# Sparse attention: TensorE's instructions of the heads held in the order of the program

## The chip, the cores and the metric

The kernel runs on one core of a Trainium2 chip. The metric is the device time of one execution in microseconds (us). The engines are TensorE (PE; its weight loads are listed apart as PEld), VectorE (DVE), ScalarE (ACT), GpSimd (POOL) and SyncE (SP), which here issues the DMAs.

## What is computed

A decoder trunk of two layers, for 256 tokens of 1024 features in float32. Layer 0 is half a SwiGLU step, stick-breaking attention, and half a SwiGLU step. Then one set of keys and values for sparse attention is derived. Layer 1 is half a SwiGLU step, native sparse attention with 16 query heads over 4 groups of keys and values, and half a SwiGLU step. The part that matters here is the sparse attention:

```python
proj = hn @ w_in
q = _apply_rope(_rmsnorm(proj[..., :H * Dh], q_norm), cos, sin)
gates = jax.nn.sigmoid(proj[..., H * Dh:])
p_c = softmax(where(valid_c, q @ k_c, NEG))       # 15 compressed keys
o_s = _nsa_selected(q, sel_idx, k_s, v_s)         # selected blocks
o_w = _nsa_window(q, k_w, v_w)                    # window of 512 keys
o = gates[0] * (p_c @ v_c) + gates[1] * o_s + gates[2] * o_w
h = h + o @ w_out
```

With 256 tokens there are four blocks of 64 keys and up to eight may be selected, and the window is longer than the sequence, so the selected and the window branch both attend causally to all keys, each with keys and values of its own.

## The kernel before

**Number format.** Products of float32 are made of three matmuls of the type fp32r (`mm3`, lines 159 to 162): each operand is split into a high part, the rounded copy made by ACT, and a low part, the remainder made by DVE. Weights arrive by DMA in units of 128 x 1024, and `pump` (L114, L116) splits a unit ahead of its use.

**What sets the order.** The program is written with a tile framework. Each instruction is traced with the tiles that it reads and writes; a scheduler then puts the instructions of each engine into one fixed order, by its own model of when each is ready and by a priority that follows the order of tracing. Semaphores are added behind that. On the chip every engine works through its fixed list; an instruction that has to wait holds what stands behind it. A tile taken from a pool with a tag and a number of buffers waits until an earlier occupant of the buffer has been read for the last time. PSUM has eight banks: the tag `acc` has four, `z` two and `aux` two.

**The sparse attention, `nsa`.** The queries and gates are projected in three blocks (`proj_block`, tile `qp`). The 16 heads, in groups `sc` of four, then pass through these steps:

- `q_trans` (L950 on): for a pair of heads, four transposes into one `aux` bank (tile `qTp`, L958), which ACT copies to `qs` (L960).
- `scores(n)`: eight matmuls (L973) into two banks. They hold a mask, the scores of 16 compressed keys, of the selected branch and of the window branch. DVE takes maxima and scales them (L990 to L993); ACT makes the exponentials of the four parts with their sums (L996, L1001) and copies the compressed scores to `cs` (L998); DVE inverts the sums (L1005); POOL multiplies by gates (L1006) and scales the probabilities P in two multiplications (L1009). Heads 0 and 2 take banks of the tag `z`, all others two of `acc`.
- `cmp_soft(sc)`: the softmax of the compressed branch for four heads (L1015 to L1025, POOL, DVE and ACT).
- `cmp_trans(sc)`: two transposes of it into an `aux` bank (tile `ct`, L1031), evacuated by ACT and DVE (L1033, L1034).
- `ptrans(n)`: the probabilities of a head, for each of two branches (b0, b1) three transposes into an `aux` bank (tile `pt`, L1049), evacuated as a high part by ACT (L1051) and a low part by DVE (L1052) into `PT`. For every second pair of heads `PT` lies in the no longer needed tiles `hTh_m` and `hTl_m`.
- `values(k)`: six matmuls (tile `O`, lines 160 to 162 through `mm3`) for two heads and one branch; every fourth call adds six matmuls of the compressed branch and has ACT and DVE evacuate `O` to the output tile `hTh_o`, `hTl_o` (L1072, L1073).
- `chunk(k)` and `mm`: the output projection (tile `o`), eight chunks over the features, whose four accumulators `oo` take all four `acc` banks.

The order of the program behind the projection is scores(3), ptrans(1), q_trans of three pairs, scores(4), and then fifteen turns:

```python
for n in range(1, 16):
    if n == 3: q_trans(2, (5,))
    if n == 6: q_trans(2, (6, 7))
    if n % 4 == 1: cmp_soft(sc)
    if n % 4 == 3: cmp_trans(sc)
    if n + 1 < 16: ptrans(n + 1)
    if n + 4 < 16: scores(n + 4)
    if n >= 12: chunk(n - 12)
    values(n - 1)
values(15)
```

(Two lines that raise the limit of split weights and split one unit are left out here.) Before the change this order only gives the priorities: the scheduler lays single matmuls of one step between those of another. After `values(15)` come the rest of the output projection and the last SwiGLU half.

Of the kernel before, what the change touches and what calls it, by code (L numbers as in the profile page):

```python
# [16 lines left out]
P = 128  # L17
# [116 lines left out]
def build(tc, ctx, a, out):  # L134
    nc = tc.nc


    pr = ctx.enter_context(tc.tile_pool(name="pr", bufs=1, side="right"))
# [20 lines left out]
    def mm3(o, xh, xl, wh, wl, start, stop):  # L159
        nc.tensor.matmul(o, xh, wh, start=start, stop=False, skip_group_check=True)  # L160
        nc.tensor.matmul(o, xh, wl, start=False, stop=False, skip_group_check=True)  # L161
        nc.tensor.matmul(o, xl, wh, start=False, stop=stop, skip_group_check=True)  # L162
# [731 lines left out]
    def nsa(hT, rs, post, targets, st):  # L894
        kD, V, vcB = st["kD"], st["V"], st["vcB"]
        tc.keep_in_program_order(nc.scalar.preload_act_table_set("natural_log_exp_and_others"))
        with tc.tile_pool(name="ns", bufs=1) as sp:
# [6 lines left out]
            qw, Pm, PT, cs, pcT, Ox = {}, {}, {}, {}, {}, {}  # L904
            heads = [(2 * sc + i, hh) for sc in range(4) for hh in range(2) for i in range(2)]

            def q_evac(b, o):

                n = 2 * len(Q_BLOCKS[b])
                h0 = 2 * Q_BLOCKS[b][0]  # L910
                w = qw[b] = sp.tile([P, 2, 6, 2, DH], F32, tag="qw", bufs=2, name="qw")
                sq = sp.tile([P, 2, 6, DH], F32, tag="qsq", bufs=1, name="qsq")[:, :, 0:n, :]
                for t in range(2):
                    ov = o[t][:, 0:n * DH].rearrange("p (n d) -> p n d", d=DH)
                    nc.vector.scalar_tensor_tensor(w[:, t, 0:n, 1, :], ov, rs[t][:, 0:1],
                                                   st["qg"].unsqueeze(1).to_broadcast([P, n, DH]),
                                                   op0=OP.mult, op1=OP.mult)
                    nc.scalar.activation(sq[:, t], ov, AF.Square, scale=rs[t][:, 0:1])
                    if b == 0:
                        nc.scalar.activation(gt[:, t, :], o[t][:, 256:304], AF.Exp, scale=rs[t][:, 2:3])  # L920
                hi, qv = w[:, :, 0:n, 0, :], w[:, :, 0:n, 1, :]
                c, sn = [cst[:, x:x + 32].rearrange("p (t i) -> p t i", t=2).unsqueeze(2) for x in (C_COS, C_SIN)]
                t1, t2 = [sp.tile([P, 2, 6, 16], F32, tag=f"qr{i}", bufs=1, name="qr")[:, :, 0:n, :] for i in range(2)]
                nc.vector.tensor_tensor(t1, qv[:, :, :, 0:16], c.to_broadcast([P, 2, n, 16]), op=OP.mult)
                for i, j in ((0, 8), (8, 0)):
                    nc.vector.tensor_tensor(t2[:, :, :, i:i + 8], qv[:, :, :, j:j + 8],
                                            sn[:, :, :, i:i + 8].to_broadcast([P, 2, n, 8]), op=OP.mult)
                nc.vector.tensor_tensor(qv[:, :, :, 0:16], t1, t2, op=OP.add)
                nc.scalar.activation(hi.bitcast(R), qv, AF.Copy)
                nc.vector.tensor_tensor(qv, qv, hi, op=OP.subtract)  # L930
                r = rq[:, :, h0:h0 + n]

                v, y, z = [sp.tile([P, 2, 8], F32, tag=f"qn{i}", bufs=2, name="qn")[:, :, 0:n] for i in range(3)]
                nc.vector.tensor_reduce(v, sq, axis=AX.X, op=OP.add)
                nc.vector.tensor_scalar(v, v, 1.0 / DH, EPS, op0=OP.mult, op1=OP.add)
                nc.scalar.activation(y, v, AF.Ln)
                nc.scalar.activation(y, y, AF.Exp, scale=-0.5)
                nc.gpsimd.tensor_tensor(z, y, y, op=OP.mult)
                nc.gpsimd.tensor_tensor(z, z, v, op=OP.mult)
                nc.gpsimd.tensor_scalar(z, z, -0.5, 1.5, op0=OP.mult, op1=OP.add)  # L940
                nc.gpsimd.tensor_tensor(r, y, z, op=OP.mult)
                if b == 0:
                    gf = gt.rearrange("p t c -> p (t c)")
                    nc.vector.tensor_scalar(gf, gf, 1.0, None, op0=OP.add)
                    nc.vector.reciprocal(gf, gf)
                    for t in range(2):
                        gc = gt[:, t, :].rearrange("p (n r) -> p n r", r=3)[:, :, 0]
                        nc.vector.tensor_scalar(gc, gc, cst[:, C_IND + t:C_IND + t + 1], None, op0=OP.mult)

            def q_trans(b, ps_=None):  # L950
                for i, p in enumerate(Q_BLOCKS[b]):
                    if ps_ is not None and p not in ps_:
                        continue
                    a_ = aux("qTp")
                    for hh in range(2):
                        for t in range(2):
                            c = hh * 256 + t * P
                            nc.tensor.transpose(a_[:, c:c + P], qw[b][:, t, 2 * i + hh, :, :].rearrange("p x d -> p (x d)"),  # L958
                                                ident)
                    nc.scalar.activation(qs[:, 2 * p:2 * p + 2, :], a_.rearrange("p (n s) -> p n s", n=2), AF.Copy)  # L960

            def scores(n, banks=accs):
# [7 lines left out]
                sb, sa = banks("S")  # L970

                def mm(o, q, k, start=False):
                    nc.tensor.matmul(o, q, k, start=start, stop=False, skip_group_check=True)  # L973

                both = lambda k: k.rearrange("p (t c) -> p t c", t=2)[:, :, 0:256]
                sv = sb.rearrange("p (t c) -> p t c", t=2)
# [50 lines left out]
            def cmp_trans(sc):  # L1027
                a_ = aux("ct")
                e = cs[sc].rearrange("p t n i -> p t (n i)")
                for t in range(2):  # L1030
                    nc.tensor.transpose(a_[0:64, t * P:(t + 1) * P], e[:, t, :], ident)  # L1031
                x = pcT[sc] = [sp.tile([64, 256], R, tag=f"pcT{y}", bufs=1, name="pcT") for y in "hl"]
                nc.scalar.activation(x[0], a_[0:64, 0:256], AF.Copy)  # L1033
                nc.vector.tensor_tensor(x[1], a_[0:64, 0:256], x[0].bitcast(F32), op=OP.subtract)  # L1034

            def ptrans(n):
                pr = Pm.pop(n)
                m, i = divmod(n, 2)
                for b in range(2):
                    if i == 0:  # L1040
                        k = 2 * m + b
                        if k % 4 < 2:
                            PT[k] = [sp.tile([P, 768], R, tag=f"PT{y}", bufs=2, name="PT") for y in "hl"]
                        else:
                            PT[k] = [x.rearrange("p a b -> p (a b)")[:, (k % 2) * 768:(k % 2) * 768 + 768]
                                     for x in (hT[0], hT[1])]
                    a_ = aux("pt")
                    for c, s0 in ((0, b * P), (P, 256 + b * 256), (2 * P, 384 + b * 256)):
                        nc.tensor.transpose(a_[:, c:c + P], pr[:, s0:s0 + P], ident)  # L1049
                    x = [y[:, i * 384:i * 384 + 384] for y in PT[2 * m + b]]  # L1050
                    nc.scalar.activation(x[0], a_[:, 0:384], AF.Copy)  # L1051
                    nc.vector.tensor_tensor(x[1], a_[:, 0:384], x[0].bitcast(F32), op=OP.subtract)  # L1052

            def values(k):

                m, br = divmod(k, 2)
                sc, hh = divmod(m, 2)
                ag = sc // 2
                if k % 4 == 0:
                    Ox[sc] = zbank("O")  # L1060
                o = Ox[sc].rearrange("p (i s) -> p i s", i=2)
                x = [y.rearrange("p (i s) -> p i s", i=2) for y in PT.pop(k)]
                for b in range(2):
                    c = slice(0, 256) if b == 0 else slice(256, 384)
                    v = [y[:, ag, br, b, hh * 64:hh * 64 + P] for y in V]
                    mm3(o[:, :, b * P:256], v[0], v[1], x[0][:, :, c], x[1][:, :, c], k % 4 == 0 and b == 0, False)
                if k % 4 < 3:
                    return
                for i in range(2):
                    mm3(o[:, i, :], vcB[0][:, ag, i, :], vcB[1][:, ag, i, :], pcT[sc][0], pcT[sc][1], False, True)  # L1070
                hi, lo = [oT[y][:, 2 * sc:2 * sc + 2, :] for y in range(2)]
                nc.scalar.activation(hi, o, AF.Copy)  # L1072
                nc.vector.tensor_tensor(lo, o, hi.bitcast(F32), op=OP.subtract)  # L1073
# [33 lines left out]
            def chunk(k):  # L1107
# [3 lines left out]
                W.done()  # L1111
                W.pump()

            scores(3)
            ptrans(1)
            q_trans(1)
            scores(4)
            for n in range(1, 16):
# [18 lines left out]
                    chunk(n - 12)  # L1137
                values(n - 1)
            values(15)
            for k in range(4, 7):  # L1140
                for hf in range(2):
                    mm(k, 0, hf)
                W.pump()
# [171 lines left out]
```

## Time and profile before

| What | Value |
|---|---|
| median of 3 runs | 1042.96 us (1042.79 to 1043.17) |
| profiled execution, its time | 1043.2 us |
| its span, first to last instruction | 1041.1 us |
| PE busy | 1030.7 us (99%) |
| DVE, ACT, POOL busy | 659.6, 583.0, 101.5 us |
| mean granted clock of TensorE | 0.997 |
| first scores of the sparse attention | 755.3 us after the span's start |
| first pt transpose of head 1 | 772.1 us |
| last matmul of `values(15)` ends | about 838.4 us |

In the profile, a row of the timeline gives the start in us, the duration, engine, line, operation, output and inputs, shape and count; in brackets stands the idle time before it and what ended it. Matmuls overlap, and their ends are modelled, so the distance from start to start says what one costs. A row of the stretches gives, for each engine, the busy us and the number of instructions, then the granted clock of TensorE (1.00 is full), the share of time in which the DMA engines were busy, and GB/s. Line numbers are those of the kernel before.

### The profile page before, as it was taken

The page shows a single profiled execution, that of the slowest core. Times are in us where ns is not written, and L with a number is a line of the kernel's source. Part 1 is how long each engine was busy: PE and PEld are TensorE (multiplying, and loading weights), DVE is VectorE, ACT ScalarE, POOL GpSimd, SP SyncE. Part 2 cuts the span into 40 slices and gives each one's busy share as a digit, 9 for nine tenths or more (in the row PEclk, how much of TensorE's full clock was granted, in tenths as well). Part 3 has the DMA queues.
Part 4 walks back from the last instruction along what each step waited for, and adds up shares of the span by engine and source line. Part 5 has one row for each costly group of instructions (what it writes and reads, how often), then busy time and mean ns, then how long its engine had stood idle before and what let it go on. Part 6 is the DMA issues. An engine that isn't in the chain of part 4 may idle for free.

```text
span 1041.1 us, 14030 instructions
## 1 busy us (share of the span) xinstructions
PE 1030.7 (99%) x5207; PEld 866.6 (83%) x5207; DVE 659.6 (63%) x924; ACT 583.0 (56%) x939; POOL 101.5 (10%) x148
## 2 busy tenths in 40 slices
PE   9999999999999999999999999999989999999998
PEld 6888888899988888888888888888977888888887
DVE  6755554788977556544776586554888665555542
ACT  6645443687866544543665565543689745454431
POOL 0000000121100000000006310000155400000000
PEclk9999999999999999999999999999989999999999
DMA  9865666444335565565555567565440136565651
GB/s 342 270 186 181 195 188 199 161 144 142 104 119 187 179 192 184 189 192 193 165 180 181 182 209 260 176 186 158 156 141 18 42 99 221 176 191 184 187 176 41
DMA packets 51332, 178.98 MB, mean 172 GB/s; under 512 B 5824, under 2 KB 6848, under 8 KB 51264
## 3 DMA queue, kind: packets, MB, share of 16 engines
q1 hardware_dynamic: 50976, 177.93, 52.8%
q8 instruction: 41, 0.67, 0.3%
q14 instruction: 27, 0.22, 0.1%
q10 hardware_dynamic: 288, 0.16, 0.0%
HBM read 177.02 MB, written 1.05 MB: 171 GB/s over the span
## 4 chain that ended last, share of the span: by engine, by line
PE 95%; DVE 2%; ACT 1%; issue 1%; DMA 0%; SPq 0%; DVEq 0%
PE a L160 15%; PE a L162 15%; PE a L161 15%; PE o L160 9%; PE o L162 9%; PE o L161 9%; PE gTp L384 2%; PE S L973 2%; PE kv L160 1%; PE kv L162 1%; PE kv L161 1%; PE hTp L274 1%; PE a L405 1%; PE pt L1049 1%; PE b L405 1%; PE qk L515 1%
## 5 line engine op out<-in xcount | busy, mean ns | idle before, releaser
L116 DVE TENSOR_TENSOR wl<-wraw,wh 128x1024 fp32r<-128x1024 f32 (+2 forms) x330 | 402.0, 1223 | 268.0 <-ACT wh L114 259.4
L114 ACT ACTIVATE wh<-wraw 128x1024 fp32r<-128x1024 f32 (+2 forms) x332 | 346.0, 1050 | 277.2 <-PE a L162 127.7
L160 PE MATMUL a<-wh,hTh_f 128*128 128x512 f32 x528 | 209.3, 396 | 0.0
L162 PE MATMUL a<-wh,hTl_f 128*128 128x512 f32 x528 | 206.0, 390 | 0.0
L161 PE MATMUL a<-wl,hTh_f 128*128 128x512 f32 x528 | 205.8, 390 | 0.0
L162 PEld LDWEIGHTS a<-wh,hTl_f 128*128 128x128 f32 x528 | 99.1, 188 | 21.1
L161 PEld LDWEIGHTS a<-wl,hTh_f 128*128 128x128 f32 x528 | 99.3, 188 | 19.5
L160 PEld LDWEIGHTS a<-wh,hTh_f 128*128 128x128 f32 x528 | 99.2, 188 | 19.6
L376 ACT ACTIVATE sil<-a,rstd 128x256 f32<-128x256 f32 x86 | 40.9, 477 | 71.3 <-PE a L162 66.0
L160 PE MATMUL o<-wh,gTh0f 128*128 128x512 f32 x192 | 73.9, 385 | 0.0
L161 PE MATMUL o<-wl,gTh0f 128*128 128x512 f32 x192 | 73.6, 383 | 0.0
L162 PE MATMUL o<-wh,gTl0f 128*128 128x512 f32 x192 | 73.5, 383 | 0.0
L160 PE MATMUL o<-wh,gTh1f 128*128 128x512 f32 (+1 forms) x160 | 61.8, 386 | 0.0
L161 PE MATMUL o<-wl,gTh1f 128*128 128x512 f32 (+1 forms) x160 | 61.3, 383 | 0.0
L162 PE MATMUL o<-wh,gTl1f 128*128 128x512 f32 (+1 forms) x160 | 61.3, 383 | 0.0
L377 DVE SCALAR_TENSOR_TENSOR g<-a,rstd,sil 128x256 f32<-128x256 f32 x86 | 41.3, 481 | 30.9 <-ACT sil L376 30.7
L251 POOL TENSOR_TENSOR rstd<-rss,mhalf 128x1 f32<-128x1 f32 x12 | 7.7, 645 | 507.5 <-DVE rss L249 507.5
L160 PE MATMUL a<-wh,hTh 128*128 128x512 f32 x144 | 56.9, 396 | 0.0
L162 PE MATMUL a<-wh,hTl 128*128 128x512 f32 x144 | 56.0, 390 | 0.0
L161 PE MATMUL a<-wl,hTh 128*128 128x512 f32 x144 | 55.9, 390 | 0.0
L162 PEld LDWEIGHTS o<-wh,gTl0f 128*128 128x128 f32 x192 | 36.0, 188 | 7.2
L161 PEld LDWEIGHTS o<-wl,gTh0f 128*128 128x128 f32 x192 | 36.1, 188 | 7.0
(309 smaller groups left out, 1768.3 us busy)
## 6 DMA issues: line engine op xcount, KB each, us to landing
wraw<-in_f2i SPq DMA_DIRECT2D x88, 512.0 KB, 3.6
wraw<-in_f1i SPq DMA_DIRECT2D x84, 512.0 KB, 4.5
wraw<-in_f1o SPq DMA_DIRECT2D x44, 512.0 KB, 3.6
wraw<-in_f2o SPq DMA_DIRECT2D x44, 512.0 KB, 3.6
wraw<-in_sbqk SPq DMA_DIRECT2D x16, 512.0 KB, 3.5
wraw<-in_kv SPq DMA_DIRECT2D x12, 512.0 KB, 3.5
wraw<-in_sbv SPq DMA_DIRECT2D x8, 512.0 KB, 4.3
wraw<-in_sbo SPq DMA_DIRECT2D x8, 512.0 KB, 3.5
```

Of the source, the lines that this page charges most:

```text
L114: nc.scalar.activation(hi[:, 0:n], raw[:, 0:n], AF.Copy)
L116: e.tensor_tensor(lo[:, 0:n], raw[:, 0:n], hi[:, 0:n].bitcast(F32), op=OP.subtract)
L160: nc.tensor.matmul(o, xh, wh, start=start, stop=False, skip_group_check=True)
L161: nc.tensor.matmul(o, xh, wl, start=False, stop=False, skip_group_check=True)
L162: nc.tensor.matmul(o, xl, wh, start=False, stop=stop, skip_group_check=True)
L274: nc.tensor.transpose(p[:, c * P:(c + 1) * P], h[:, t, k:k + P], ident)
L376: nc.scalar.activation(sil, o[t][:, 0:256], AF.Silu, scale=rs[t][:, 0:1])
L377: nc.vector.scalar_tensor_tensor(g, o[t][:, 256:512], rs[t][:, 0:1], sil, op0=OP.mult, op1=OP.mult)
L384: nc.tensor.transpose(p[:, c * 256 + t * P:c * 256 + (t + 1) * P], gs[j, t][:, c * P:(c + 1) * P], ident)
L405: nc.tensor.matmul(o[j][t], x[:, k, t * P:(t + 1) * P], w, start=k == 0 and i == 0, stop=k == 7 and i == 2, skip_group_check=True)
L515: nc.tensor.matmul(oi, wh[:, c], xh, start=k == 0 and q == 0, stop=False, skip_group_check=True)
L973: nc.tensor.matmul(o, q, k, start=start, stop=False, skip_group_check=True)
```

## The change

A flag `order` is set while the program from `scores(3)` to `values(15)` is traced. While it is set, every matmul and transpose of these steps, and of the chunks that lie among them, passes through `tc.keep_in_program_order`. That gives the instruction an edge to the instruction traced before it on the same engine: the scheduler may not place it earlier. It is an edge for the scheduler alone; no semaphore wait comes with it. The work on other engines is traced as before and is still placed by the scheduler, and so is TensorE's work traced before and behind the flagged part. `nsa` gets an `mm3` of its own that issues the same three matmuls in the same order.

```diff
+            order = [False]
+
+            def pe(ins):
+
+                if order[0]:
+                    tc.keep_in_program_order(ins)
+                return ins
+
+            def mm3(o, xh, xl, wh, wl, start, stop):
+                for x, w, i in ((xh, wh, 0), (xh, wl, 1), (xl, wh, 2)):
+                    pe(nc.tensor.matmul(o, x, w, start=start and i == 0, stop=stop and i == 2, skip_group_check=True))
...
-                            nc.tensor.transpose(a_[:, c:c + P], qw[b][:, t, 2 * i + hh, :, :].rearrange("p x d -> p (x d)"),
-                                                ident)
+                            pe(nc.tensor.transpose(a_[:, c:c + P],
+                                                   qw[b][:, t, 2 * i + hh, :, :].rearrange("p x d -> p (x d)"), ident))
...
-                    nc.tensor.matmul(o, q, k, start=start, stop=False, skip_group_check=True)
+                    pe(nc.tensor.matmul(o, q, k, start=start, stop=False, skip_group_check=True))
...
-                    nc.tensor.transpose(a_[0:64, t * P:(t + 1) * P], e[:, t, :], ident)
+                    pe(nc.tensor.transpose(a_[0:64, t * P:(t + 1) * P], e[:, t, :], ident))
...
-                        nc.tensor.transpose(a_[:, c:c + P], pr[:, s0:s0 + P], ident)
+                        pe(nc.tensor.transpose(a_[:, c:c + P], pr[:, s0:s0 + P], ident))
...
+            order[0] = True
             scores(3)
             ptrans(1)
             q_trans(1)
...
                 values(n - 1)
             values(15)
+            order[0] = False
             for k in range(4, 7):
```

## The prediction

> **What bounds the kernel now.** I read first the page's busy times and its chain, then busy time in stretches of 6 us through the sparse attention, then TensorE's waits there, and last the timeline of single engines.
>
> ```profile
> PE 1030.7 (99%) x5207; PEld 866.6 (83%) x5207; DVE 659.6 (63%) x924; ACT 583.0 (56%) x939; POOL 101.5 (10%) x148
> ...
> PE 95%; DVE 2%; ACT 1%; issue 1%; DMA 0%; SPq 0%; DVEq 0%
> ```
>
> TensorE (PE) sets the end: time is won only where it idles or runs slowly, and lost wherever the change makes it wait. The whole kernel offers 1041.1 - 1030.7 = 10.4 us of idle time. The stretches of the heads (PE, PEld, DVE, ACT, POOL, granted clock, DMA):
>
> ```profile
> 768.00:774.00 6.00, 2.89 (x15) 1.83 (x13) 6.00 (x16) 6.00 (x20) 3.61 (x4) 0.85 0.33 109
> ...
> 786.00:792.00 6.00, 6.00 (x40) 4.64 (x39) 5.13 (x17) 5.72 (x23) 3.63 (x6) 1.00 0.00 0
> 792.00:798.00 6.00, 6.00 (x43) 5.10 (x43) 4.74 (x16) 5.80 (x23) 4.56 (x9) 1.00 0.01 1
> 798.00:804.00 6.00, 5.10 (x38) 4.09 (x37) 4.74 (x15) 5.77 (x21) 2.93 (x6) 1.00 0.00 0
> 804.00:810.00 6.00, 6.00 (x41) 4.89 (x40) 4.45 (x12) 5.70 (x23) 3.75 (x7) 1.00 0.01 3
> 810.00:816.00 6.00, 6.00 (x41) 4.95 (x39) 5.33 (x18) 4.08 (x16) 2.58 (x6) 1.00 0.00 0
> ```
>
> In the steady part PE is full in all rows but one, and ScalarE (ACT) is busy 5.7 to 5.8 of 6 us until 810. The two are almost equally loaded, so a wait of one soon reaches the other, and what keeps PE full is that the scheduler lays other ready work between the pieces of one head. The waits of PE from 750 to 850 us are few:
>
> ```profile
> PE pt L1049 <- POOL P L1009: 1.7, 1, 1.7
> PE S L973 <- ACT qsq L918: 0.8, 1, 0.8
> PE ct L1031 <- DVE hTl_m L1052: 0.6, 1, 0.6
> PE O L160 <- ACT PT L1051: 0.6, 1, 0.6
> PE O L160 <- ACT hTh_m L1051: 0.3, 1, 0.3
> ```
>
> The first two stand at the start of the pinned stretch and are followed by a slow clock:
>
> ```profile
> 771.00:772.00 1.00, 0.00 (x0) 0.00 (x0) 1.00 (x3) 1.00 (x3) 1.00 (x2) 1.00 0.52 209
> 772.00:773.00 1.00, 0.83 (x3) 0.46 (x3) 1.00 (x3) 1.00 (x6) 0.08 (x1) 0.61 0.00 0
> ...
> 778.00:779.00 1.00, 1.00 (x5) 0.82 (x5) 0.79 (x2) 0.38 (x2) 0.92 (x2) 0.50 0.67 127
> 779.00:780.00 1.00, 1.00 (x9) 0.90 (x7) 0.04 (x1) 0.60 (x1) 1.00 (x2) 0.98 0.92 377
> ```
>
> The granted clock is 0.5 until 779 and full after it. Half of about 6.3 us is 3.2 us lost.
>
> **The change part by part.** It adds no instruction and no semaphore, and moves nothing on SP, so no DMA changes place. What changes is the order on PE from scores(3) to values(15): turn n of the loop becomes [transposes of queries or of the compressed scores], the six transposes of head n+1, scores(n+4), [one chunk of the output projection], values(n-1). The first instruction that cannot go now holds back all that follows. The costs on PE, from starts to the next start:
>
> ```profile
> 795.52 0.30 PE L973 MATMUL S<-mns,identb 128*128 128x288 bf16 x1
> ...
> 796.63 0.48 PE L160 MATMUL O<-PT,Vh 128*128 128x512 f32 x1
> ...
> 797.77 0.60 PE L958 MATMUL qTp<-cst,qw 128*128 128x128 f32 x4
> 798.21 0.29 PE L973 MATMUL S<-mns,identb 128*128 128x288 bf16 x1
> ```
>
> Scores take 1.11, values 1.14, the four transposes of a query pair 0.44 us. Now one buffer of the tag aux, which has two: from its filling to its next filling.
>
> ```profile
> 802.79 0.49 PE L1049 MATMUL pt<-cst,P 128*128 128x128 f32 x3
> ...
> 804.56 0.82 PE L1049 MATMUL pt<-cst,P 128*128 128x128 f32 x6
> 805.21 0.27 PE L973 MATMUL S<-mns,identb 128*128 128x256 bf16 x1
> ```
> ```profile
> 803.38 0.49 ACT L1051 ACTIVATE PT<-pt 128x384 fp32r<-128x384 f32 x1 [0.23 <-PE pt L1049]
> ```
> ```profile
> 803.90 0.56 DVE L1052 TENSOR_TENSOR PT<-pt,PT 128x384 fp32r<-128x384 f32 x1 [0.31 <-ACT PT L1051]
> ```
>
> Six transposes take 0.65 us, so three take 0.33 and the two of ct about 0.22. The buffer turns in 804.56 - 802.79 = 1.77 us with ACT free at once. A query pair (one evacuation, no DVE step) and ct (smaller evacuations) turn in about 1.4 us, my estimate from these parts.
>
> 1. *Runs of transposes.* In the trace other work lies between them; in the new order it may not.
> - Turn 3 has qT5, ct, pt4 b0, pt4 b1 in a row. b0 needs qT5's buffer, 1.4 us after it, and PE has 0.44 + 0.22 = 0.66 of work: 0.74 wait; b1 needs ct's, at 0.44 + 1.4 = 1.84 against 1.73: 0.11.
> - Turn 6 has qT6, qT7, pt7 b0, b1: 1.4 - 0.88 = 0.52, and 0.11.
> - Turns 7 and 11 have ct, b0, b1: 1.4 - 0.22 - 0.33 = 0.85 each.
>
> Sum 0.85 + 0.63 + 1.7 = 3.2 us. (The last ct, turn 15, is followed by a chunk and costs nothing.)
>
> 2. *ACT's queue in front of the evacuations.* The 1.4 us hold for a free ACT. One head's exponentials hold it this long:
>
> ```profile
> 784.28 0.52 ACT L996 ACTIVATE P<-S,nm,rq 128x128 f32<-128x128 f32 x1
> ...
> 786.33 0.68 ACT L960 ACTIVATE qs<-qTp 128x512 fp32r<-128x512 f32 x1
> ```
>
> That is 2.05 of about 3.3 us per head (786 to 810 serves about seven heads). An evacuation meets such a block 62% of the time and waits half of it: 0.64 us, in four runs 2.5 us. Bounds: 0 (the scheduler puts the evacuation first) and 4 x 2.05 = 8.2. I take 2.5.
>
> 3. *Scores to transposes of the same head.* In the new order PE comes to pt(h) after values and two full turns from the end of scores(h): 1.14 + 2 x (0.65 + 1.11 + 1.14) = 6.9 us. In the trace of head 8:
>
> ```profile
> 788.25 0.30 PE L973 MATMUL S<-mns,identb 128*128 128x288 bf16 x1
> ...
> 789.91 0.28 PE L973 MATMUL S<-mns,identb 128*128 128x256 bf16 x1
> ```
> ```profile
> 796.19 1.61 POOL L1009 TENSOR_TENSOR P<-P,nm 128x256 f32<-128x256 f32 x2
> ```
>
> P is ready 797.80 - 790.19 = 7.6 us after its scores, while the scheduler takes its transposes at 802.79, 5 us later still. So some 0.7 us are missing in turns without extra work, about five of twelve: 3.5 us if ACT lags as now, nothing if the later scores find a shorter queue. I take a third, 1.1 us; the wait of chunk(0) for the score banks of heads 14 and 15 is the same chain without POOL and is counted in it.
>
> 4. *The start.* pt1 comes at 772.14 as before, since everything ahead of it keeps its order. So I expect the gap, and the slow clock, to stay.
>
> ```profile
> 772.14 0.83 PE L1049 MATMUL pt<-cst,P 128*128 128x128 f32 x3 [1.73 <-POOL P L1009]
> 773.55 0.79 PE L160 MATMUL O<-PT,Vh 128*128 128x512 f32 x1 [0.58 <-ACT PT L1051]
> 774.14 0.84 PE L1049 MATMUL pt<-cst,P 128*128 128x128 f32 x3
> 774.78 1.06 PE L958 MATMUL qTp<-cst,qw 128*128 128x128 f32 x4
> ...
> 779.08 0.37 PE L973 MATMUL S<-kDh,qs 128*128 128x272 f32 x1
> ```
>
> Now five fillings of aux (pt1 twice, three query pairs) stand in a row; values(0) and the first part of values(1), which lie between them today (about 1.3 us at full clock), go behind. By my estimate pt1 b1 then starts some 0.6 us sooner, the query pairs at about 774.6, 775.7 and 776.9, each a buffer's turn behind the last but one and 0.85 long at half clock, and the scores of head 4 at 778, not 779.1. That is 1.1 us sooner with 1.3 us of values owed: +0.2, and +0.5 for one evacuation behind exponentials. I take +0.7 us; bounds 0, and 1.7 if the slow stretch of 6.8 us lasts half as long again (3.4 us at half speed). [...]
>
> 5. *Waits that go.* The three later waits of the list, 0.6 + 0.6 + 0.3 = 1.5 us. Modelled ends hide more:
>
> ```profile
> 790.27 0.49 PE L1049 MATMUL pt<-cst,P 128*128 128x128 f32 x3
> 790.70 0.38 PE L160 MATMUL O<-pcT,vcBh 64*128 64x256 f32 x1
> ...
> 794.03 0.49 PE L1049 MATMUL pt<-cst,P 128*128 128x128 f32 x3
> 794.27 0.48 PE L161 MATMUL O<-PT,Vh 128*128 128x512 f32 x1
> ```
>
> The same three transposes hold PE 0.43 and 0.24 us; some six to eight such places make 1.5 us. Gain at most 3.0, taken whole.
>
> Sum: 3.2 + 2.5 + 1.1 + 0.7 - 3.0 = +4.5 us. Against the profiled execution's 1043.2 us (span 1041.1) this is 1047.7; the median of the runs, 1042.96, is 0.2 lower, so 1047.5. After the heads PE is full again and nothing gives it back.
>
> **The rivals.**
> - *Hidden anyway (no change, 1043 to 1045).* The scheduler's order already is close to the program's, and most stalls replace the 3.0 us of point 5: 3.2 + 0.7 - 3.0 = +0.9, 1043.9. For it: ACT has 2.2 us of idle in 804 to 816, so evacuations might come in time. Against: the rows before 804.
> - *Faster (1040).* With six transposes in one piece and scores always ahead of values, ACT gets its work in the order in which it is needed, evacuations never queue, and the waits of point 5 go: 1043.0 - 3.0 = 1040.0. It decides where a buffer of aux turns in less than the 0.55 to 0.88 us of transposes laid between. Against it stands the row of 1.77 us; even the shorter turns would have to be halved. A larger gain needs the gap at 769 to 772 to close, and nothing ahead of it moves.
> - *Much slower (1053).* Points 2 and 3 near their upper bounds: 3.2 + 6 + 2 + 1.7 - 3.0 = +9.9. PE and ACT then wait for each other in turn, and ACT loses in idling what it cannot make up at 95% load.
>
> **How the numbers follow.** Forecast (1045 to 1050.5) 0.47; much slower 0.15; no change 0.21; faster 0.17. About 0.2% (2.1 us) is what a measurement of this kernel can tell from none. Faster by more 0.17, within 0.21, slower 0.62. The range takes in the faster case's middle and the much slower one's: 1040.0 to 1053.5.
>
> **What would show it.** On PE: pieces in program order, no values between the transposes from 772 to 779; waits in front of the second pt of turns 7 and 11, and of pt4 and pt7, released by the DVE or ACT evacuation of ct and qT; scores(4) not before 777; clock 0.5 again from 772; the last values later by 4 to 5 us against the first pt1. I am wrong if PE's idle time in 772 to 850 does not rise by about 4 us, if the clock stays full there, or if pt waits are released by nothing but POOL.

## The result and the profile after

The changed kernel takes 1057.74 us (median of four runs, 1055.95 to 1058.57) against 1042.90 for the kernel before beside it: 14.8 us more, ratio 1.0139 [1.0123, 1.0156]. The direction was forecast, the size was not: the prediction said +4.5 and allowed for at most 1053.5.

The profiled execution took 1058.57 us, with a span of 1056.6. The page's busy times and the first line of its chain:

```profile
PE 1035.8 (98%) x5207; PEld 871.0 (82%) x5207; DVE 658.5 (62%) x924; ACT 582.6 (55%) x939; POOL 102.6 (10%) x148
...
PE 90%; DVE 3%; issue 3%; ACT 2%; POOL 1%; DMA 1%; SPq 0%; POOLq 0%; DVEq 0%; ACTq 0%
```

TensorE (PE) has the same 5207 instructions. Its idle time has grown from 10.4 to 1056.6 - 1035.8 = 20.8 us, and its busy time by 1035.8 - 1030.7 = 5.1 us. So the 15.5 us of the span are 10.4 of waiting and 5.1 of the same work done more slowly. Both stand in the stretch of the heads. The same 6 us windows as before the change (PE, PEld, DVE, ACT, POOL, granted clock, DMA):

```profile
768.00:774.00 6.00, 2.65 (x18) 1.91 (x15) 6.00 (x15) 5.95 (x22) 4.00 (x4) 0.80 0.41 135
...
786.00:792.00 6.00, 3.29 (x17) 2.60 (x14) 1.92 (x6) 3.86 (x15) 3.62 (x6) 0.73 0.02 3
792.00:798.00 6.00, 6.00 (x29) 4.99 (x28) 2.98 (x11) 2.93 (x11) 0.94 (x3) 0.71 0.00 0
798.00:804.00 6.00, 4.92 (x35) 4.12 (x34) 4.33 (x13) 3.90 (x14) 4.12 (x8) 1.00 0.01 1
804.00:810.00 6.00, 3.82 (x17) 2.94 (x16) 1.72 (x4) 3.73 (x13) 1.81 (x3) 0.65 0.00 0
810.00:816.00 6.00, 4.97 (x26) 4.06 (x25) 2.99 (x9) 3.28 (x12) 1.81 (x3) 0.78 0.01 3
...
766.00:855.00 89.00, 75.04 (x416) 61.90 (x415) 54.74 (x139) 58.95 (x191) 38.23 (x67) 0.88 0.14 43
```

The last row is the whole stretch. ScalarE (ACT), which was busy 5.7 us of each 6 until 810 before, is now busy 2.9 to 3.9 in the rows from 786 to 816, and the clock, full there before, falls to 0.65 to 0.78 in four of these five rows. In four of the five PE and ACT both idle (from 792 to 798 PE is busy throughout, but slow); the rows of turn 3 below show them waiting for each other.

PE's waits from 750 to 870 us (total, times, longest):

```profile
PE pt L1061 <- DVE pcT L1046: 4.7, 3, 2.1
PE pt L1061 <- POOL P L1021: 3.9, 2, 2.8
PE pt L1061 <- ACT qs L972: 2.7, 3, 1.9
PE qTp L970 <- DVE cm L1033: 1.1, 1, 1.1
PE pt L1061 <- DVE hTl_m L1064: 0.7, 1, 0.7
PE pt L1061 <- DVE PT L1064: 0.6, 1, 0.6
```

They sum to 13.7 us. 2.8 and 0.55 of it are at the start, where the kernel before has 0.80, 1.73 and 0.58. The other 10.3 lie in the turns, 9.3 of them in turns 3, 6, 7 and 11, the four that the prediction named. Most (4.7 + 2.7 = 7.4 us) are waits of `pt` for the copy of a buffer of `aux` that held `ct` (its low half, `pcT`) or a query pair (`qs`). Turn 3, on PE, ACT and VectorE (DVE), the columns being start, length, engine, line, operation and, in brackets, the idle time before it:

```profile
785.96 0.38 PE L1043 MATMUL ct<-cst,cs 128*64 128x128 f32 x2
786.90 0.52 PE L1061 MATMUL pt<-cst,P 128*128 128x128 f32 x3 [0.56 <-ACT qs L972]
789.57 0.90 PE L1061 MATMUL pt<-cst,P 128*128 128x128 f32 x3 [2.15 <-DVE pcT L1046]
790.26 0.45 PE L985 MATMUL S<-mns,identb 128*128 128x288 bf16 x1
```
```profile
786.16 0.60 ACT L972 ACTIVATE qs<-qTp 128x512 fp32r<-128x512 f32 x1
786.66 0.45 ACT L1008 ACTIVATE P<-S,nm,rq 128x128 f32<-128x128 f32 x1
...
788.14 0.59 ACT L1013 ACTIVATE P<-S,nm,rq 128x256 f32<-128x256 f32 x1
...
788.68 0.38 ACT L1045 ACTIVATE pcT<-ct 64x256 fp32r<-64x256 f32 x1
...
793.67 0.46 ACT L1008 ACTIVATE P<-S,nm,rq 128x128 f32<-128x128 f32 x1 [2.61 <-DVE nm L1003]
```
```profile
788.85 0.18 DVE L1017 RECIPROCAL nm<-nm 128x4 f32<-128x4 f32 x1 [2.55 <-ACT P L1013]
789.10 0.42 DVE L1046 TENSOR_TENSOR pcT<-ct,pcT 64x256 fp32r<-64x256 f32 x1
```

For comparison, the same place on PE before the change:

```profile
785.46 0.38 PE L1031 MATMUL ct<-cst,cs 128*64 128x128 f32 x2
785.68 0.29 PE L973 MATMUL S<-mns,identb 128*128 128x288 bf16 x1
...
787.33 0.49 PE L1049 MATMUL pt<-cst,P 128*128 128x128 f32 x3
```

There the scheduler lets scores follow `ct` at once, and `pt` comes 1.9 us later without a wait. The rows after the change are the whole loss in small. `ct` is done at 786.34, but its copy stands in ACT's list behind one head's exponentials, all of them, 786.66 to 788.68. On DVE the second copy stands behind a reciprocal that waits for the same exponentials. The second `pt` of turn 3 needs that buffer, and behind it, in the pinned order, stand scores that have no wait of their own when they come (790.26). PE does nothing for 2.15 us; then ACT, whose next scores come late, does nothing for 2.61.

On ACT the kernel before has the same order in this place:

```profile
786.80 0.56 ACT L996 ACTIVATE P<-S,nm,rq 128x128 f32<-128x128 f32 x1
...
788.85 0.42 ACT L1033 ACTIVATE pcT<-ct 64x256 fp32r<-64x256 f32 x1
```

There too `ct` waits for a whole head's exponentials, and its buffer is filled again only at 790.27, 4.8 us after 785.46, against 3.6 us with the change. It cost nothing, because PE had scores and values to do meanwhile. So in turn 3 the pin did not move the copy; it took away the work that covered it. In turns 7 and 11 the copy of `ct` stands right behind a head's exponentials in both kernels as well.

Turn 6 has such a wait for the second query pair: its copy follows a head's exponentials, and `pt` waits 1.94 us. Here the list did change: the kernel before copies both query pairs together, in a row of two at 798.95.

```profile
806.14 0.23 ACT L1013 ACTIVATION_READ_ACCUMULATOR P<-S,nm,rq 128x1 f32 x1
806.23 0.62 ACT L972 ACTIVATE qs<-qTp 128x512 fp32r<-128x512 f32 x1
```
```profile
806.91 0.90 PE L1061 MATMUL pt<-cst,P 128*128 128x128 f32 x3 [1.94 <-ACT qs L972]
```

What the gap does next, in windows of 1 us:

```profile
786.00:787.00 1.00, 0.44 (x5) 0.20 (x3) 0.18 (x1) 0.93 (x5) 0.54 (x2) 1.00 0.00 0
787.00:788.00 1.00, 0.42 (x3) 0.18 (x3) 0.00 (x0) 1.00 (x6) 1.00 (x2) 1.00 0.09 16
788.00:789.00 1.00, 0.00 (x0) 0.00 (x0) 0.15 (x1) 1.00 (x6) 0.28 (x1) 0.86 0.00 0
789.00:790.00 1.00, 0.43 (x2) 0.43 (x3) 0.93 (x3) 0.44 (x2) 0.81 (x3) 0.50 0.00 0
...
795.00:796.00 1.00, 1.00 (x9) 0.99 (x8) 0.06 (x1) 1.00 (x5) 0.78 (x2) 0.73 0.00 0
```

The granted clock drops to a half at the end of 788 and comes back in 795. A mean of 0.86 puts the drop at 788.72 and one of 0.73 the return at 795.54, 6.8 us later. Turn 6 brings a second stretch, from 805.8 to 812.6. PE is busy 5.97 and 5.69 us in the two; half of that at a granted clock of 0.50 is a loss of 3.0 + 2.8 = 5.8 us.

From the first chunk on (834.1 us) PE is full again, busy 26.00 of the 26 us from 834 to 860 at a clock of 1.00. The first matmul of the remaining projection starts at 853.95, against 838.43 before, and this difference of 15.5 us stays to the end.

### The profile page after: what moved, and what is told of

It reads as the page before. It is cut to its first block, busy times and chain, and to the rows that moved or that the text cites. A ratio compares the mean times of both kernels' runs of the same rounds, so it can differ in the third digit from the quotient of the medians.

```text
span 1056.6 us, 14043 instructions
## 1 busy us (share of the span) xinstructions
PE 1035.8 (98%) x5207; PEld 871.0 (82%) x5207; DVE 658.5 (62%) x924; ACT 582.6 (55%) x939; POOL 102.6 (10%) x148
## 4 chain that ended last, share of the span: by engine, by line
PE 90%; DVE 3%; issue 3%; ACT 2%; POOL 1%; DMA 1%; SPq 0%; POOLq 0%; DVEq 0%; ACTq 0%
PE a L160 15%; PE a L162 14%; PE a L161 14%; PE o L160 8%; PE o L162 8%; PE o L161 8%; PE o L917 2%; PE gTp L384 2%; PE O L917 2%; PE S L985 1%; PE kv L160 1%; PE kv L162 1%; PE kv L161 1%; PE hTp L274 1%; PE pt L1061 1%
```

## The experiments

The theory was: the pinned order costs time only because PE now stops at a buffer of `aux` whose copy stands behind a head's exponentials, and because the gap trips the clock. The rivals were: the start pays; the order of turns 3, 6, 7 and 11 is what is bad, whatever the copies do; the clock alone is the larger part. Each kernel is compared with the kernel before, run beside it (medians 1042.9 to 1043.5). Differences to the change are worked out from the ratios, a hundredth of the ratio being 10.4 us; the change itself is 14.5 us by that count.

**Pin the start alone.** The flag is set down again right behind scores(4).

```diff
             order[0] = True
             scores(3)
...
             scores(4)
+            order[0] = False
```

> Only the start is pinned (scores of head 3 to scores of head 4); the fifteen turns are left to the scheduler. Theory 1 (the time is lost where several fillings of aux follow each other in the turns, and to the slow clock behind these waits): the start costs under 1 us, 1042.5 to 1044. Rival (the loss is spread over the whole stretch, because PE and ACT now work in lockstep): the start has a share by its length, 7 of 82 us, so 1044 to 1045. If the start were the cause: over 1050.

Measured: 1043.36 us, ratio 0.9997 [0.9988, 1.0006]. Nothing measurable. But this pins less than the change does: the values, traced behind the flag, still lie between the transposes of the start:

```profile
773.53 0.70 PE L917 MATMUL O<-PT,Vh 128*128 128x512 f32 x1 [0.78 <-ACT PT L1063]
```

So the start's own price is read from the traces of before and after. `ct` of turn 3 starts at 785.96 against 785.46, with one matmul of the values (0.24 us) less done by then, and 0.4 us of the delay lie ahead of the start (first `pt` at 772.55 against 772.14): 0.5 + 0.24 - 0.4 = 0.3 us. The loss lies in the turns.

**Spread the transposes over the turns, still pinned.** Query pair 5 goes to turn 2, pair 6 to turn 5, and pair 7 stays in turn 6; these and `ct` come behind the scores of their turn.

```diff
-                if n == 3:
-                    q_trans(2, (5,))
-                if n == 6:
-                    q_trans(2, (6, 7))
...
-                if n % 4 == 3:
-                    cmp_trans(sc)
...
+                if n in (2, 5, 6):
+                    q_trans(2, ({2: 5, 5: 6, 6: 7}[n],))
+                if n % 4 == 3:
+                    cmp_trans(sc)
```

> All is pinned as in the changed kernel, but the order of the program is another: the query transposes and the ct transposes stand behind the scores of their turn, one per turn (turns 2, 5, 6; ct in 3, 7, 11, 15), so that no turn begins with three or four fillings of aux. Theory 1: the waits of turns 3, 6, 7 and 11 (9.3 us) and the two slow stretches (5.7 us) mostly go: 1043 to 1047. Rival (any fixed order costs, since nothing can be laid between): 1053 to 1057.

Measured: 1053.62 us, 1.0098 [1.0081, 1.0115], 4.3 us better than the change but a miss, and in the range of the rival. The waits moved to the other filling of the buffer:

```profile
PE ct L1043 <- DVE PT L1064: 4.3, 3, 1.7
PE qTp L970 <- DVE hTl_m L1064: 3.3, 2, 1.9
```

Now `ct` and the query pair wait for the copies of `pt`, which stand behind exponentials in their turn. Where PE reaches `aux` matters less than that it must stop there. The two experiments that follow speak against the rival: they keep a fixed order too.

**Same PE order, copies out of `aux` first.** The scheduler's priority of the copies of `pt`, `ct` and the query pairs (ACT and DVE) is raised by EARLY = 300; PE's order is that of the change.

```diff
+                prio = tc.cur_priority
+                tc.cur_priority = prio - EARLY
                 nc.scalar.activation(x[0], a_[0:64, 0:256], AF.Copy)
                 nc.vector.tensor_tensor(x[1], a_[0:64, 0:256], x[0].bitcast(F32), op=OP.subtract)
+                tc.cur_priority = prio
```

> The order on PE stays that of the changed kernel; only the copies that empty aux (ACT and DVE, of pt, ct and qTp) get a higher priority in the scheduler, so that they stand ahead of the exponentials in ACT's list where both are ready. Theory 1 with the queue on ACT as its larger part: waits of turns 3, 6, 7, 11 fall from 9.3 to about 4 us and the clock stays full: 1044 to 1049. If the waits come from the length of the evacuation itself, not its place in the queue: 1054 to 1058.

Measured: 1046.98 us, 1.0038 [1.0023, 1.0053], as expected: 10.5 us of the 14.5 are gone with PE's order untouched. ACT in the same turn 3, and the waits for `ct`'s copy over the whole stretch:

```profile
786.95 0.45 ACT L1012 ACTIVATE P<-S,nm,rq 128x128 f32<-128x128 f32 x1
...
787.49 0.38 ACT L1051 ACTIVATE pcT<-ct 64x256 fp32r<-64x256 f32 x1
787.77 0.44 ACT L1012 ACTIVATE P<-S,nm,rq 128x128 f32<-128x128 f32 x1
```
```profile
PE pt L1068 <- DVE pcT L1052: 1.8, 3, 0.6
```

The copy now goes in between two exponentials of one head; the waits of `pt` for it fall from 4.7 to 1.8 us.

**More banks instead, no priority.** `ct` and the query pairs of the turns take a buffer of the tag `z`, which the sums of the values otherwise have to themselves, so `pt` has `aux` alone. PE's order is the same as in the change.

```diff
-                    a_ = aux("qTp")
+                    a_ = (zbank if b == 2 else aux)("qTp")
...
-                a_ = aux("ct")
+                a_ = zbank("ct")
```

> Pinned with the order of the changed kernel; ct and the query transposes of the turns take a bank of the tag z, one of which is free between two outputs O, and not one of aux. ACT's list is not touched by a priority. Theory: the waits for ct's and qT's copies (4.7 and 2.7 us) go and with them both slow stretches (5.7 us): 1045 to 1049; what is left is pt behind pt and P. Rival (the copies behind exponentials hold PE up all the same, at the next pt): 1052 to 1056.

Measured: 1049.16 us, 1.0057 [1.0042, 1.0072], 8.6 us better than the change and just above what was expected. Two reliefs with nothing in common but the buffer's turn each take most of the loss away, at the same order of PE. That shows the buffer's turn as the place where the pinned order loses its time. `pt` still waits for the copies of earlier `pt`, three times (once at the start), up to 1.3 us:

```profile
PE pt L1061 <- DVE PT L1064: 2.8, 3, 1.3
```

**Only the copies of `ct` and query pairs first, in the turns.** The same two lines stand around the copies of `ct`; those of `pt` keep their priority.

```diff
+            early = [0]
...
+                    prio = tc.cur_priority
+                    tc.cur_priority = prio - early[0]
                     nc.scalar.activation(qs[:, 2 * p:2 * p + 2, :], a_.rearrange("p (n s) -> p n s", n=2), AF.Copy)
+                    tc.cur_priority = prio
...
             scores(4)
+            early[0] = 300
```

> The order on PE of the changed kernel; only the copies of ct and of the query transposes, and only in the turns, go ahead of the exponentials; those of pt stay where they were. Theory (the long waits are those for ct's and qT's copies): 1046 to 1050, most of the gain of the priority on all copies. Rival (the copies of pt matter as much): 1051 to 1055.

Measured: 1050.27 us, 1.0070 [1.0056, 1.0084], just above what was expected. These copies carry half of the loss, 7.2 us. The other 3.3 us that the third experiment saved belong, by subtraction, to `pt`'s own copies and to those of the start, which this kernel leaves alone.

**Keep the clock up.** Behind the first `pt` of heads 4 and 7 (turns 3 and 6) PE gets 32 small matmuls into a part of the bank that nobody reads. The computation is unchanged.

```diff
+                    if b == 0 and n in (4, 7):
+                        for _ in range(32):
+                            pe(nc.tensor.matmul(a_[:, 384:512], identb, identb, start=True, stop=True,
+                                                skip_group_check=True))
```

> As the changed kernel, with 32 small matmuls (128 columns, bf16, into a part of the pt bank that nobody reads) behind the first half of the transposes of heads 4 and 7, where PE waits about 2 us and the clock falls. Extra work, about 2 x 1.8 us, in the two waits of 2.15 and 1.94 us. If the slow clock behind these waits costs 5.7 us: 1051 to 1053. If the clock is only a mark of the wait and costs nothing of its own: 1057 to 1060.

Measured: 1054.70 us, 1.0109 [1.0094, 1.0124]: 3.1 us better than the change, whose interval it just touches, and between the two expectations. The row that fills the gap of turn 3, and two windows:

```profile
787.56 1.95 PE L1064 MATMUL pt<-identb 128*128 128x128 bf16 x32
```
```profile
786.00:792.00 6.00, 5.07 (x55) 4.35 (x54) 2.48 (x9) 4.28 (x15) 3.63 (x6) 1.00 0.00 0
792.00:798.00 6.00, 6.00 (x44) 5.29 (x42) 3.40 (x11) 5.22 (x21) 2.64 (x5) 1.00 0.01 1
```

The clock stays full in the turns (1.00 in every stretch of 6 us from 780 to 840), and `pt` comes when its buffer does (0.37 us of wait are left), so the gap does cause the slow stretches. Between the two profiled executions the fill is worth 1056.6 - 1051.8 = 4.8 us, close to the 5.1 of slower work; but that sets the slowest of four executions of the change (mean clock 0.990, the others 0.992 to 0.994) against the fastest with the fill. By the ratios it is 3.1. The rest of the loss stays: the clock is no more than about a third of it.

**Spread and copies first, pinned.** The edits of the second and third experiment together.

> Pinned, with the spread order of the program and with the copies out of aux ahead of the exponentials. Theory (what is left are fillings of aux that wait for a copy queued behind a head's exponentials; the order on PE sets how many, ACT's list how long): both together give 1042 to 1045.5, below each alone (1053.6 and 1047.0). Rival (any order fixed on PE costs some us because nothing can be laid between): about 1047, no better than the second alone.

Measured: 1043.49 us, 1.0007 [0.9998, 1.0016], as expected, with a clock of 1.00 in the trace. With both, the pinned order costs and brings nothing that can be told.

**The same two reliefs without the pin.** The priorities, and the banks, on the kernel before.

> The kernel before, nothing pinned, with the copies out of aux ahead of the exponentials. Theory: the wait of 2.8 us at 769 to 772 shrinks, as in the pinned kernel with this priority (PE busy 4.1 of 6 us there, 2.9 before), and with it the slow stretch behind it (3.2 us): 1037 to 1041. Rival (the scheduler's order needs the exponentials early, to have work to lay between): 1042 to 1046.

Measured: 1046.06 us, 1.0032 [1.0020, 1.0043]: slower, against the expectation. The gap at 769 to 772 closes, but the price is paid behind it. Head 3's exponentials begin at 776.50, against 771.88 in the kernel before, as ACT and DVE now serve copies and query work first; head 3's probabilities are late, and the clock now goes down there, to a mean of 0.61 from 780 to 786, where it was 1.00 before:

```profile
781.55 0.69 PE L1056 MATMUL pt<-cst,P 128*128 128x128 f32 x2 [1.60 <-POOL P L1013]
```
```profile
768.00:774.00 6.00, 5.32 (x36) 3.92 (x35) 6.00 (x13) 6.00 (x19) 4.08 (x5) 1.00 0.41 143
...
780.00:786.00 6.00, 4.45 (x17) 3.50 (x18) 3.12 (x11) 3.10 (x12) 4.19 (x7) 0.61 0.26 87
```

> The kernel before, nothing pinned, with ct and the later query transposes in banks of the tag z. Theory: the scheduler already lays other work between, so little to win: the three later waits of 1.5 us at most, 1041 to 1043. If the shortage of aux costs the kernel before as well: under 1040.

Measured: 1043.03 us, 0.9998 [0.9989, 1.0008], at the upper end of what was expected. Neither relief is a gain by itself. What they gave in the pinned order was the repair of what the pin had broken.

**Can the pinned order win?** First spread and priorities from turn 1 on only, so that the start stays as it was; then both everywhere, with the last part of the work on the third query block (`q_evac(2)`: rotation, low parts, norms) moved back in priority by LOW = 100; and that last edit, with the priorities, on the order of the scheduler.

```diff
             scores(4)
+            early[0] = 300
```
```diff
+                qprio = tc.cur_priority
+                tc.cur_priority = qprio + (LOW if b == 2 else 0)
                 hi, qv = w[:, :, 0:n, 0, :], w[:, :, 0:n, 1, :]
...
                 nc.gpsimd.tensor_tensor(r, y, z, op=OP.mult)
+                tc.cur_priority = qprio
```

> Pinned, with the spread order; the copies out of aux go ahead of the exponentials only from the first turn on, and the start is left as in the changed kernel. In the kernel with the priority from the start on, the exponentials of head 3 came 4.8 us later and PE waited 1.7 and 0.6 us for their banks. Theory: without that, 1039 to 1042, at or below the kernel before. Rival (the start's gap and its slow clock, which return, cost as much as those waits): 1042.5 to 1045.

> Pinned, spread, all copies first also at the start, and the last part of the third query block's work (rotation, low parts, norms; not needed before turn 2) given a low priority, so that the maxima and exponentials of head 3 are not behind it. Theory (the start's gap of 2.8 us and the slow clock behind it can go if the copies and head 3 are both served first): 1037 to 1041. Rival (DVE and ACT are full from 766 to 776, so something else comes late instead): 1042 to 1046.

> The kernel before, nothing pinned, order of the program as before, with the two priorities of the run before this one (copies out of aux first, the third query block's last part late). If the order on PE matters for itself even where no copy is late: 2 us or more away from the pinned kernel with the same priorities. If only the late copies mattered: within 1.5 us of it, 1037 to 1043.

Measured: 1043.74 us, 1.0006 [0.9997, 1.0015]; 1043.24, 1.0002 [0.9993, 1.0011]; and 1041.69, 0.9987 [0.9978, 0.9996]. The pinned kernels end at the time of before, whichever repair they get: both theories missed, and the rivals had it right. The third, whose order is the scheduler's, is the fastest here. Its gain of 0.13% is below the 0.2% that the prediction set as what can be told, but its interval ends short of 1, and all its eleven runs (1041.19 to 1042.11) lie below the eleven of the second (1042.77 to 1044.39). So with the same priorities the scheduler's order is still about 1.5 us ahead, just between the two expectations: the late copies were nearly all that the order mattered for, but perhaps not all. The second kernel's longest group of waits shows where the pinned order stops next, at the score banks, for exponentials:

```profile
PE S L992 <- ACT P L1020: 2.1, 3, 0.8
```

## Why the prediction was right and wrong

| step | predicted, us | measured |
|---|---|---|
| 1 and 2, waits at `aux` in turns 3, 6, 7, 11 | 3.2 + 2.5 = 5.7 | 9.3, of it 7.4 for `ct` and query pairs |
| 3, probabilities late | 1.1 | one wait of 1.08, turn 10 |
| 4, start | 0.7 (0 to 1.7) | 0.3 |
| clock in the turns | not in the sum | 3.1 by the ratios, 4.8 between two traces |
| 5, waits that go | -3.0 | at most 1.5 seen to go |
| all | +4.5 | +14.8 |

The rows are not a full account; the split that adds up is the page's, 10.4 us of idling and 5.1 of slower work in a span of 15.5 more.

*Right.* The four turns were named, with the second `pt` as the waiting instruction and the copies of `ct` and the query pairs as what it waits for (7.4 of the 9.3 us). Scores(4) start at 778.01 (forecast 778), at half clock (0.50) as forecast. That the times agree so closely is luck: the first `pt` came 0.4 us later than forecast, and the three query pairs took 3.07 us, not 3.4.

```profile
774.94 3.28 PE L970 MATMUL qTp<-cst,qw 128*128 128x128 f32 x12
778.01 0.45 PE L985 MATMUL S<-mns,identb 128*128 128x288 bf16 x1
```

The lateness of 1.1 us behind scores was met once, about its size. After the heads nothing is given back.

*The step that failed is point 2*: "An evacuation meets such a block 62% of the time and waits half of it: 0.64 us". That averages over chance meetings. In the fixed list of ACT there is no chance: the copy has one place, and in turns 3 and 6 it is behind the block, so the wait is the whole of it, 2.0 us. If point 1 is left at its 3.2, the term came out at 9.3 - 3.2 = 6.1 and not 2.5, inside its bounds of 0 and 8.2. And the 1.4 us that point 1 took for a turn of the buffer held for a free ACT only; in turn 3 `ct` needs from 785.96 to 789.52, 3.6 us. The trace before already had the copy of `ct` behind a whole head's exponentials, and its buffer out for 4.8 us; the prediction read the turn from a `pt` that ACT served at once. The experiments confirm it: 7.2 us come back when the copies of `ct` and the query pairs alone change places, 10.5 with those of `pt` and of the start.

*Left out was the clock away from the start.* Point 4 gave a longer slow stretch a price, 1.7 us for half as long again, but only at the start. In turns 3 and 6 the clock fell during waits of 2.15 and 1.94 us behind a whole block of exponentials, and stayed at 0.50 for 6.8 us, as long as at the start. Points 1 and 2 spread 5.7 us over four turns, 1.4 us each, and asked of none whether it trips the clock; the same fault thus cost a second time, by the 3 to 5 us that the fill gave back.

*Point 5 was counted whole.* The three waits that it named (1.5 us) are gone from PE's list. The other 1.5 us, hidden in modelled ends, can't be seen as won: with half of the busy time at half clock taken off, PE's busy time is about 1030.7 - 3.1 = 1027.6 us before and 1035.8 - 8.4 = 1027.4 after, an estimate from the two traces.

*The start* cost 0.3 of the 0.7 us forecast, and its slow stretch lasted 6.8 us (771.64 to 778.46), as before the change (772.21 to 779.04). No run shows the 1.7 us that point 4 and the sum of "much slower" allowed for a longer one.

Of the rivals, "much slower" had the mechanism. It said that PE and ACT wait for each other in turn and that ACT loses in idling, and the row of 2.61 us of idle ACT shows it. It had 0.15 of the chance and 1053, as it took 6 us for point 2 and again no clock in the turns. The "faster" rival named what decides, the turn of a buffer against the transposes laid between, and the row of 1.77 us argued rightly against it: even with the copies first, at 1043.49, the pinned order wins nothing.

What stays open: why the scheduler, with the pin, puts a block of exponentials between the two query copies of turn 6 is not seen in a trace. It was only shown that a higher priority or a bank of its own undoes the wait.

## What to carry to other kernels

Pinning one engine's order takes away the slack that let it go around a late buffer; before pinning, look in the trace where the copies that free each buffer already stand in the other engines' lists, and price a wait by the whole block ahead of it, not by its average. If an order must be pinned, give those copies priority or a bank of their own in the same edit: here that was worth 10.5 and 8.6 us of 14.5. Look at the granted clock around each wait of the engine that sets the end: here it fell to a half during waits of 2.15 and 1.94 us and stayed there for 6.8 us each time.

## What the hardware showed that was not expected

A gap need not be empty for the clock to fall, and behind a wait of 1.66 us it stayed full. In the changed kernel the granted clock falls at 771.64, 788.71 and 805.78, and stands at 0.50 for 6.8 us each time. The first two rows show the 3.41 us (half the length of such a slow stretch) ahead of the two falls in the turns. The other two show stretches of the same length from the kernel with its transposes spread, which hold its waits of 1.66 and 1.94 us (PE alone: busy us, count, granted clock, DMA share, GB/s):

```profile
785.30:788.71 3.41, 1.56 (x13) 1.00 0.03 5
...
802.37:805.78 3.41, 1.68 (x11) 1.00 0.00 0
```
```profile
787.15:790.56 3.41, 1.75 (x11) 1.00 0.00 0
...
797.39:800.80 3.41, 1.47 (x11) 1.00 0.00 0
```

Before the two falls PE had thus worked for 1.56 and 1.68 us. Behind the third stretch the clock is 1.00 in every us up to 796; behind the fourth it falls, to a mean of 0.73 from 798 to 804. What decides between the two was not shown.

The four executions of the change took longer the lower their mean clock was: 1055.95 us at 0.994, 1057.18 at 0.993, 1058.30 at 0.992, 1058.57 at 0.990. How their slow stretches differ was not shown: only one of the four left a trace.
